# Seven half-size products for eight in the down projection of one decoder step

## The chip, the core and the metric

The kernel runs on one core of a Trainium2 chip. Its engines work side by side, each through its own queue in order: TensorE (PE) multiplies matrices into the accumulation memory PSUM; VectorE (DVE) and ScalarE (ACT) do element-wise work and can read PSUM; GpSimd (POOL) does element-wise work between tiles of the on-chip memory SBUF; SyncE (SP) issues the transfers (DMA). The metric is the time of one execution on the device in microseconds (us), from three runs for the kernel before.

## The reference

One layer of a hybrid decoder: a combined input projection, sparse attention and a recurrent branch, an output projection with a first layer norm, and then the feed-forward part, in which the change lies. There are 1032 tokens (1024 of the prompt, 8 of the sample), 1024 channels and 4096 hidden units:

```python
x1 = _layer_norm(DN_ALPHA * x + mix, ln1_g, ln1_b)
hid = jnp.square(jax.nn.relu(x1 @ w_up + b_up))
x2 = _layer_norm(DN_ALPHA * x1 + hid @ w_down + b_down, ln2_g, ln2_b)
```

The products are wanted in nearly full float32 precision. The kernel splits each operand into a high part in the shorter format that PE multiplies (fp32r) and a low part, and forms high·high + high·low + low·high: three matmuls for each one of the mathematics.

## The kernel before

Channels and hidden units lie on the 128 partitions, tokens along the free dimension. The feed-forward part (functions `g_mlw` and `g_mlp`) goes through 16 chunks of 256 hidden units. A chunk's weights are two tiles of w_up and two of w_down, 512 KB each; `g_mlw` loads each into a buffer `raw`, ACT writes its high part (L2226) and POOL its low part (L401 in the helper `gtt`, which cuts a row into four pieces of 256). They land in `wm`, one tile per chunk, in two places that take turns, so that a chunk's weights are prepared while the chunk before it is multiplied.

The tokens are cut into three groups of 384, 384 and 264 (`GROUPS`). `up` (L2249) multiplies, for one group and one half `f` of the chunk's hidden units, eight slices of the input by three products, 24 matmuls in one PSUM bank (L2260 to L2262). ACT applies bias and relu (L2266), DVE squares (L2269), ACT takes the high part of the hidden values (`hh`, L2273) and DVE the low part (`hl`, L2277). `down` (L2282) forms for one group and one slice `m` of 128 output channels six matmuls (two halves by three products, L2293 to L2295) in a bank, and DVE adds the bank to the running sum `MX` in SBUF (L2304). A chunk so has 144 matmuls up and 144 down, and 24 additions. The last chunk has groups of its own (`LAST`), and the second layer norm (`g_ln2`) runs behind it; its tiles lie in `late`.

The order on every engine is made before the run by a planner in the kernel (class `Weave`): each stream yields chains of operations with a cost on an engine and with the buffers they take and give back, and the planner emits, one by one, the operation that can start first, with a bonus per stream to break near ties. Four banks (`mm`) serve `up` and `down`; two double banks (`pr`, tiles named `pair`) serve transposes. What it emits is fixed: at run time every engine works its list off in order, and an instruction that waits holds back all behind it.

## Time and profile before

| what | value |
|---|---|
| median of 3 runs | 1443.86 us (1443.5 to 1445.07) |
| profiled execution | 1449.08 us, span from first to last instruction 1447.3 us |
| PE, DVE, ACT, POOL busy over the span | 95%, 60%, 44%, 36% |
| mean granted clock of PE | 0.986 of full speed |
| feed-forward part | first matmul at 693.1 us, chunk 15 from 1373.4 us, last matmul at 1431.4 us |

The span counts from the first instruction to the last; the remaining 1.8 us lie around it. PE is shown by its recorded instructions, whose ends are modelled: one matmul's record overlaps the next one's, so the distance between two starts is what a matmul costs, not its recorded length. The records of the other engines also run a little past the point where the next instruction can start.

### The profile page before, as it was taken

To read this page: it belongs to the slowest core of one execution; us is meant where nothing else is said; L and a number is where in the kernel's file an instruction comes from. 1 tells how busy PE (TensorE), PEld (TensorE's weight loads), DVE (VectorE), ACT (ScalarE), POOL (GpSimd) and SP (SyncE) were. 2 spreads that over 40 slices of the span, in tenths; PEclk is the share of its full clock that TensorE was granted. 3 is DMA by queue.
4 is the path that set the end of the run, shared out by engine and by line. 5 is a ranking of instruction groups with operands and counts; after the bars stand their busy time and mean duration, and the time that the engine had idled before them with its cause. 6 is when DMAs were issued, how large, how long until landed. Compare 5 with 4: busy or idle time off the path is not lost.

```text
span 1447.3 us, 24305 instructions
## 1 busy us (share of the span) xinstructions
PE 1377.3 (95%) x9529; PEld 1278.7 (88%) x9529; DVE 862.1 (60%) x1969; ACT 635.1 (44%) x1206; POOL 518.7 (36%) x675
## 2 busy tenths in 40 slices
PE   8999998899889998999999999999999999999995
PEld 7987787789876776768999999999999999999995
DVE  7388877688988578658744433344333443334457
ACT  5377998788334566556521122211222112221123
POOL 1213645454316685432431133311333113331124
PEclk9999999999999999999999999999999999999998
DMA  6122431013224353241111111111111111111012
GB/s 216 54 79 66 145 83 42 18 44 101 76 86 134 113 161 104 89 146 60 59 45 31 43 59 59 44 31 43 59 59 45 31 44 58 59 44 32 16 57 89
DMA packets 39380, 102.17 MB, mean 71 GB/s; under 512 B 6441, under 2 KB 11865, under 8 KB 39137
## 3 DMA queue, kind: packets, MB, share of 16 engines
q1 hardware_dynamic: 34144, 83.83, 17.9%
q0 software_dynamic: 5120, 16.78, 4.0%
q8 instruction: 75, 1.23, 0.4%
q14 instruction: 41, 0.33, 0.1%
HBM read 87.55 MB, written 14.62 MB: 71 GB/s over the span
## 4 chain that ended last, share of the span: by engine, by line
PE 76%; DVE 12%; ACT 7%; issue 3%; DMA 1%; POOL 1%; SPq 0%; another core or an unknown queue 0%; DVEq 0%; ACTq 0%; POOLq 0%
PE bank L2260 8%; PE bank L2261 8%; PE bank L2262 8%; PE bank L2295 8%; PE bank L2293 8%; PE bank L2294 8%; PE bank L532 4%; PE bank L533 3%; PE bank L534 3%; ACT jka L1239 3%; PE pair L1932 3%; PE bank L2032 2%; PE bank L1993 2%; DVE SC L693 2%; DVE late L2397 1%
## 5 line engine op out<-in xcount | busy, mean ns | idle before, releaser
L401 POOL TENSOR_TENSOR wm<-raw,wm 128x256 fp32r<-128x256 f32 x256 | 198.8, 807 | 481.9 <-ACT wm L2226 481.8
L2304 DVE TENSOR_TENSOR MX<-MX,bank 128x384 f32<-128x384 f32 (+2 forms) x352 | 178.6, 508 | 132.7 <-PE bank L2295 129.9
L2260 PE MATMUL bank<-X1H,wm 128*128 128x384 f32 (+2 forms) x784 | 248.2, 317 | 0.8 <-DVE MX L2304 0.8
L2261 PE MATMUL bank<-X1L,wm 128*128 128x384 f32 (+2 forms) x784 | 248.2, 317 | 0.0
L2262 PE MATMUL bank<-X1H,wm 128*128 128x384 f32 (+2 forms) x784 | 248.0, 316 | 0.0
L2293 PE MATMUL bank<-hh,wm 128*128 128x384 f32 (+2 forms) x752 | 239.4, 318 | 0.0
L2295 PE MATMUL bank<-hh,wm 128*128 128x384 f32 (+2 forms) x752 | 239.1, 318 | 0.0
L2294 PE MATMUL bank<-hl,wm 128*128 128x384 f32 (+2 forms) x752 | 238.5, 317 | 0.0
L532 PE MATMUL bank<-XH,wh 128*128 128x384 f32 (+1 forms) x600 | 200.9, 335 | 10.3 <-DVE kbs L1137 8.5
L2226 ACT ACTIVATE wm<-raw 128x1024 fp32r<-128x1024 f32 x64 | 66.9, 1050 | 296.4 <-PE bank L2295 296.4
L533 PE MATMUL bank<-XL,wh 128*128 128x384 f32 (+1 forms) x600 | 194.0, 323 | 0.8 <-DVE XL L477 0.8
L534 PE MATMUL bank<-XH,wl 128*128 128x384 f32 (+1 forms) x600 | 193.6, 323 | 0.2 <-DVE wl L513 0.2
L2269 DVE TENSOR_TENSOR r<-r 128x384 f32<-128x384 f32 (+2 forms) x98 | 53.6, 547 | 207.0 <-ACT r L2266 207.0
L2260 PEld LDWEIGHTS bank<-X1H,wm 128*128 128x128 f32 x784 | 147.5, 188 | 1.2 <-DVE MX L2304 1.0
L2262 PEld LDWEIGHTS bank<-X1H,wm 128*128 128x128 f32 x784 | 147.4, 188 | 0.0
L2261 PEld LDWEIGHTS bank<-X1L,wm 128*128 128x128 f32 x784 | 147.1, 188 | 0.0
L2294 PEld LDWEIGHTS bank<-hl,wm 128*128 128x128 f32 x752 | 141.8, 189 | 0.0
L2293 PEld LDWEIGHTS bank<-hh,wm 128*128 128x128 f32 x752 | 141.3, 188 | 0.0
L2295 PEld LDWEIGHTS bank<-hh,wm 128*128 128x128 f32 x752 | 141.2, 188 | 0.0
L2266 ACT ACTIVATE r<-bank,pvt 128x384 f32<-128x384 f32 (+2 forms) x98 | 52.9, 541 | 196.7 <-PE bank L2262 196.7
L532 PEld LDWEIGHTS bank<-XH,wh 128*128 128x128 f32 x600 | 114.6, 191 | 21.4 <-DVE kbs L1137 12.2
L401 POOL TENSOR_TENSOR wl<-raw,wh 128x256 fp32r<-128x256 f32 x92 | 77.5, 872 | 148.9 <-ACT wh L509 144.0
(419 smaller groups left out, 2491.9 us busy)
## 6 DMA issues: line engine op xcount, KB each, us to landing
raw<-in_wup SPq DMA_DIRECT2D x32, 512.0 KB
raw<-in_wdown SPq DMA_DIRECT2D x32, 512.0 KB
raw<-in_win SPq DMA_DIRECT2D x25, 512.0 KB
raw<-in_wout SPq DMA_DIRECT2D x8, 512.0 KB
zo<-in_x SPq DMA_DIRECT2D x16, 256.0 KB
zsc<-zo SPq DMA_DIRECT2D x16, 256.0 KB
z<-zsc SPq DMA_DIRECT2D x16, 256.0 KB
out_y<-late SPq DMA_DIRECT2D x16, 256.0 KB
```

The costliest lines, as they stand in the source:

```text
L401: G.tensor_tensor(out=out[:, c0:c1], in0=in0[:, c0:c1], in1=in1[:, c0:c1], op=op)
L532: T.matmul(ps[:, :n], wh[:, k, :], XH[:, k, c0:c0 + n], start=(k == 0), stop=False)
L533: T.matmul(ps[:, :n], wh[:, k, :], XL[:, k, c0:c0 + n], start=False, stop=False)
L534: T.matmul(ps[:, :n], wl[:, k, :], XH[:, k, c0:c0 + n], start=False, stop=(k == KT - 1))
L2226: S.activation(out=wts[c][:, 2 * i, 0:1024], in_=b2["f"], func=AF.Copy)
L2260: T.matmul(ps[:, :n], wh, X1H[:, k, c0:c0 + n], start=(k == 0), stop=False)
L2261: T.matmul(ps[:, :n], wh, X1L[:, k, c0:c0 + n], start=False, stop=False)
L2262: T.matmul(ps[:, :n], wl, X1H[:, k, c0:c0 + n], start=False, stop=(k == KT - 1))
L2293: T.matmul(ps[:, :n], wh, hh[:, :n], start=(f == 0), stop=False)
L2294: T.matmul(ps[:, :n], wh, hl[:, :n], start=False, stop=False)
L2295: T.matmul(ps[:, :n], wl, hh[:, :n], start=False, stop=(f == 1))
L2304: V.tensor_tensor(out=acc, in0=acc, in1=b2["ps"][:, :n], op=OP.add)
```

## The change

For chunks 1 to 14 the down product of a chunk, a 1024×256 by 256×1032 product, is taken as a 2×2 block product: w_down of the chunk is cut into A11, A12, A21, A22 (by output channels in two halves of 512 and by the two hidden halves of 128), the hidden values into B11, B12, B21, B22 (by hidden half and by tokens in two halves of 516). Eight block products would give the four result blocks; the changed kernel forms seven, A11·B11, A12·B21, S1·T1, S2·T2, S3·T3, S4·B22 and A22·T4, where S1 = A21 + A22, S2 = S1 − A11, S3 = A11 − A21, S4 = A12 − S2, and T1 to T4 are such differences of the B blocks. The sums S are made by DVE in place in the two `raw` buffers, a step of a chain that also splits all seven weight blocks (`g_mla`); the sums T are made by DVE in place in the hidden tiles `R` (`g_b`). A product has four slices `m` of 128 output channels, each of six matmuls of 258 columns into one double bank (`g_down`, L2434). Its result is added by DVE (L2446) into one of seven accumulators: four are blocks of `MX`, three (`ex`, E0 to E2) lie in the place of one weight tile; S1·T1 is added to two of them. Only after chunk 14 are the accumulators put together, by six additions of 2064 elements (`g_comb`, L2478).

Around it: the up product of these chunks uses three equal token groups of 344 and is cut in four pieces, between which the planner may set other matmuls; the up weights have one place in the place of two, so that a chunk's weights follow the ones before into the same rows when those are done; w_down blocks go through six rows that are given on from block to block (`ar`); a bank is read into two `R` tiles where it lies across the middle of the tokens. The second layer norm's parameters are loaded after the combination.

```diff
+        ST = range(1, NCH - 1)
+        NH = NT // 2
+        NG = NH // 2
+        UG = [(0, 344), (344, 344), (688, 344)]
...
+            yield "dn0"
+            for c in ST:
+                if 1 < c < ST[-1]:
+                    yield f"wt{c + 1}0"
...
+                return ([_op("SP", 0.12, l0, ["ra", "rb"]), _op("DMA", _dma(1048576))] + split_("A22", "22") + add("22", "21", "22", OP.add)
+                        + split_("S1", "22") + add("21", "11", "21", OP.subtract) + split_("A11", "11") + add("22", "22", "11", OP.subtract)
+                        + add("11", "12", "22", OP.subtract) + split_("S4", "11") + split_("S3", "21", ["rb"])
+                        + split_("A12", "12") + split_("S2", "22", ["ra"]))
...
+            prod = {"T1": ("R01", "R00"), "T3": ("R11", "R01"), "T2": ("R11", "R00"), "T4": ("R10", "R11")}.get(nme)
...
+                    for x, (w, b) in enumerate(((wh, bh), (wh, bl), (wl, bh))):
+                        for g in range(2):
+                            T.matmul(b2["pt"][:, g, 0:NG], w, b[:, g * NG:(g + 1) * NG], start=(x == 0), stop=(x == 2))
...
+                for A, B, w in (("A11", "B11", "E0"), ("A12", "B21", "11"), ("S1", "T1", ""), ("S4", "B22", "12"), ("S3", "T3", "E2"), ("S2", "T2", "E1"), ("A22", "T4", "21")):
...
+            for waits, ch in ((("dE0", "d11"), add(lambda: q(0, 0), e[0], "c11")), (("dE1",), add(e[1], e[0], "u2")),
+                              (("u2", "d12"), add(lambda: q(0, 1), e[1], "c12")), (("u2", "dE2"), add(e[2], e[1], "u3")),
+                              (("u3", "d22"), add(lambda: q(1, 1), e[2], "c22")), (("u3", "d21"), add(lambda: q(1, 0), e[2], "c21"))):
```

Up to the first up product of chunk 0 every engine's list is as before. In chunk 12, on PE, the down product before is a run of six matmuls per bank, with four banks taking turns (`hh`, `hl` are the hidden values, `wm` the weights):

```order
L2293 MATMUL bank_13126<-hh_12946,wm_12494 128x384 [waits Activation_49]
L2294 MATMUL bank_13126<-hl_12947,wm_12494 128x384
L2295 MATMUL bank_13126<-hh_12946,wm_12494 128x384
L2293 MATMUL bank_13126<-hh_12984,wm_12494 128x384
L2294 MATMUL bank_13126<-hl_12985,wm_12494 128x384
L2295 MATMUL bank_13126<-hh_12984,wm_12494 128x384
L2293 MATMUL bank_13134<-hh_12946,wm_12494 128x384 [waits DVE_49]
```

After, these are the slices 1 and 2 of chunk 9's product S2·T2, in a run of nine slices without an up product between; chunks 6 and 12 have the same run there (`bh`, `bl` are the parts of a B or T block):

```order
L2434 MATMUL pair_12642<-bh_12402,wm_7251 128x258 [waits DVE_49]
L2434 MATMUL pair_12642<-bh_12402,wm_7251 128x258
L2434 MATMUL pair_12642<-bl_12403,wm_7251 128x258 x2
L2434 MATMUL pair_12642<-bh_12402,wm_7251 128x258 x2
L2434 MATMUL pair_12650<-bh_12402,wm_7251 128x258 [waits DVE_49]
L2434 MATMUL pair_12650<-bh_12402,wm_7251 128x258
L2434 MATMUL pair_12650<-bl_12403,wm_7251 128x258 x2
L2434 MATMUL pair_12650<-bh_12402,wm_7251 128x258 x2
```

Each slice now waits for DVE to have emptied the double bank of the slice before the last: two places take turns where four did. Elsewhere most slices stand in twos with one piece of an up product (six matmuls of 344) between.

On DVE, the down product of chunk 13 before begins so (additions of banks among the last squares and subtractions of the up product):

```order
L2277 TENSOR_TENSOR hl_13506<-r_13502,hh_13505 128x264 [waits Activation_49]
L2269 TENSOR_TENSOR r_13516<-r_13516 128x264 [waits Activation_49]
L2304 TENSOR_TENSOR MX<-MX,bank_13509 128x384 [waits PE_49]
L2277 TENSOR_TENSOR hl_13527<-r_13516,hh_13526 128x264 [waits Activation_49]
L2304 TENSOR_TENSOR MX<-MX,bank_13519 128x384 [waits PE_49]
L2304 TENSOR_TENSOR MX<-MX,bank_13531 128x384 [waits PE_49]
```

After, where the hidden values of chunk 8 become complete while its first product A11·B11 is added (L2446), DVE has these in a row (L2534 squares, L2388 forms a T, L2401 forms a low part):

```order
L2446 TENSOR_TENSOR ex_7879<-ex_7879,pair_11852 128x516 [waits PE_49]
L2534 TENSOR_TENSOR r_11812<-r_11812 128x344 [waits Activation_49]
L2401 TENSOR_TENSOR bl_11880<-r_11812,bh_11879 128x516 [waits Activation_49]
L2388 TENSOR_TENSOR r_11531<-r_11812,r_11531 128x516
L2388 TENSOR_TENSOR r_11812<-r_11812,r_11487 128x516 [waits DVE_49]
L2401 TENSOR_TENSOR bl_11908<-r_11531,bh_11907 128x516 [waits Activation_49]
L2401 TENSOR_TENSOR bl_11911<-r_11812,bh_11910 128x516 [waits Activation_49]
L2388 TENSOR_TENSOR r_11728<-r_11728,r_11812 128x516
L2446 TENSOR_TENSOR ex_7879<-ex_7879,pair_11872 128x516 [waits PE_49]
L2401 TENSOR_TENSOR bl_11942<-r_11728,bh_11941 128x516 [waits Activation_49]
L2446 TENSOR_TENSOR ex_7879<-ex_7879,pair_11882 128x516 [waits PE_49]
```

Seven instructions between tiles in SBUF now stand between two additions that empty double banks; in the rows before it is one.

After chunk 14, on DVE, four of the six closing additions (L2478, 2064 elements each) stand between the additions of PE's products:

```order
L2446 TENSOR_TENSOR ex_7879<-ex_7879,pair_15009 128x516 [waits PE_49]
L2478 TENSOR_TENSOR ex_7879<-ex_7879 128x2064 [waits DVE_49]
L2478 TENSOR_TENSOR MX<-MX,ex_7879 128x4x516 [waits DVE_49]
L2478 TENSOR_TENSOR ex_7879<-ex_7879 128x2064
L2478 TENSOR_TENSOR MX<-MX,ex_7879 128x4x516 [waits DVE_49]
L2446 TENSOR_TENSOR MX<-MX,pair_15017 128x516 [waits PE_49]
```

The last of them empties the double bank that a later slice of the last product A22·T4 needs; the kernel before had no such additions.

## Rows read from the trace of the kernel before

**Rows 1.** The page, section 1: busy time, share of the span, instructions.
```profile
PE 1377.3 (95%) x9529; PEld 1278.7 (88%) x9529; DVE 862.1 (60%) x1969; ACT 635.1 (44%) x1206; POOL 518.7 (36%) x675
```

**Rows 2.** Busy time by stretch; the first line names the columns.
```profile
core 0: us, PE busy (x) PEld busy (x) DVE busy (x) ACT busy (x) POOL busy (x), PEclk, DMA share, GB/s
...
1020.00:1065.00 45.00, 45.00 (x289) 45.00 (x288) 18.65 (x36) 10.04 (x16) 12.10 (x16) 1.00 0.15 48
...
1410.00:1448.00 38.00, 21.80 (x143) 19.23 (x141) 29.42 (x49) 11.54 (x21) 18.00 (x13) 0.83 0.24 91
```

**Rows 3.** The chain that ended last, by engine.
```profile
PE 76%; DVE 12%; ACT 7%; issue 3%; DMA 1%; POOL 1%; SPq 0%; another core or an unknown queue 0%; DVEq 0%; ACTq 0%; POOLq 0%
```

**Rows 4.** Timeline of ACT: start, length, what; first weight split of chunks 5 and 6.
```profile
921.22 1.06 ACT L2226 ACTIVATE wm<-raw 128x1024 fp32r<-128x1024 f32 x1 [21.18 <-PE bank L2295]
...
966.47 1.06 ACT L2226 ACTIVATE wm<-raw 128x1024 fp32r<-128x1024 f32 x1 [21.18 <-PE bank L2295]
```

**Rows 5.** Timeline of PE: start, length; first matmul of three stretches of chunk 7.
```profile
1011.47 0.34 PE L2260 MATMUL bank<-X1H,wm 128*128 128x384 f32 x1
...
1028.25 0.28 PE L2260 MATMUL bank<-X1H,wm 128*128 128x264 f32 x1
...
1034.12 0.34 PE L2293 MATMUL bank<-hh,wm 128*128 128x384 f32 x1
```

**Rows 6.** Groups by line and shape, chunk 7 (1020 to 1065): count, busy, mean ns.
```profile
L2304 DVE TENSOR_TENSOR MX<-MX,bank 128x384 f32<-128x384 f32 x16 | 8.9, 554 | 7.1 <-PE bank L2295 6.9
...
L2304 DVE TENSOR_TENSOR MX<-MX,bank 128x264 f32<-128x264 f32 x8 | 3.4, 429 | 2.3 <-PE bank L2295 2.3
...
L2273 ACT ACTIVATE hh<-r 128x384 fp32r<-128x384 f32 x4 | 2.1, 522 | 1.9 <-DVE r L2269 1.9
...
L2273 ACT ACTIVATE hh<-r 128x264 fp32r<-128x264 f32 x2 | 0.9, 426 | 1.0 <-DVE r L2269 1.0
...
L401 POOL TENSOR_TENSOR wm<-raw,wm 128x256 fp32r<-128x256 f32 x16 | 12.4, 802 | 32.9 <-ACT wm L2226 32.9
```

**Rows 7.** Timeline of DVE: two instructions one behind the other.
```profile
990.13 0.56 DVE L2304 TENSOR_TENSOR MX<-MX,bank 128x384 f32<-128x384 f32 x1
990.60 0.43 DVE L2277 TENSOR_TENSOR hl<-r,hh 128x264 fp32r<-128x264 f32 x1
```

**Rows 8.** Timelines of PE and DVE: a product's last matmul, its addition.
```profile
1005.46 0.34 PE L2295 MATMUL bank<-hh,wm 128*128 128x384 f32 x1
...
1005.83 0.56 DVE L2304 TENSOR_TENSOR MX<-MX,bank 128x384 f32<-128x384 f32 x1 [0.49 <-PE bank L2295]
```

**Rows 9.** Timeline of SP and ACT: issue of two weight loads, read of the first.
```profile
925.19 5.33 SPq L2222 DMA_DIRECT2D raw<-in_wdown  x2
...
931.26 1.05 ACT L2226 ACTIVATE wm<-raw 128x1024 fp32r<-128x1024 f32 x1
```

**Rows 10.** Shortest, median and longest of three lines of DVE.
```profile
L2277 DVE TENSOR_TENSOR hl<-r,hh x98: 405/557/1097, 709.3 to 1414.4; 128x384 fp32r<-128x384 f32 x60, 128x264 fp32r<-128x264 f32 x32, 128x256 fp32r<-128x256 f32 x6
...
L2269 DVE TENSOR_TENSOR r<-r x98: 405/558/1451, 705.4 to 1413.4; 128x384 f32<-128x384 f32 x60, 128x264 f32<-128x264 f32 x32, 128x256 f32<-128x256 f32 x6
...
L2124 DVE TENSOR_TENSOR z<-z,bank x18: 676/686/689, 639.9 to 693.3; 128x512 f32<-128x512 f32 x16, 8x512 f32<-8x512 f32 x2
```

**Rows 11.** Timelines of DVE and POOL: a subtraction that starts during a POOL run.
```profile
1017.89 0.79 DVE L2277 TENSOR_TENSOR hl<-r,hh 128x384 fp32r<-128x384 f32 x1 [0.80 <-ACT hh L2273]
...
1017.53 3.13 POOL L401 TENSOR_TENSOR wm<-raw,wm 128x256 fp32r<-128x256 f32 x4 [1.87 <-ACT wm L2226]
```

**Rows 12.** Timelines of PE and DVE: chunk 15 begins; last matmul, last DVE group.
```profile
1373.44 0.28 PE L2260 MATMUL bank<-X1H,wm 128*128 128x264 f32 x1
...
1431.40 0.40 PE L2366 MATMUL bank<-wm,hh 128*128 128x512 f32 x1
...
1438.34 5.46 DVE L2397 TENSOR_TENSOR late<-late 128x512 f32<-128x512 f32 x5
```

More of the change, by code (lines that the diff above doesn't have):

```diff
@@ L2225, in l1 @@
                 def l1():
[L2226 removed]
+                    S.activation(out=rows()[0][:, 0:1024], in_=b2["f"], func=AF.Copy)
                 def l2():
[L2229 removed]
+                    gtt(out=rows()[1][:, 0:1024], in0=b2["f"], in1=rows()[0][:, 0:1024].bitcast(F32), op=OP.subtract)
                     W.fire(f"wt{c}{i}")
[L2231 removed]
@@ L2232, in g_mlw @@
-            for c in range(NCH):
-                if c == 1:
-                    for i in range(9):
-                        yield f"om{i}"
-                elif c:
-                    yield f"dn{c - 2}"
-                for i in range(4):
-                    yield chain(c, i), 1
-            yield f"dn{NCH - 2}"
+                rw = "raw" if c == 0 else ("rb", "ra", "ra", "rb")[i]
+                return [_op("SP", 0.06, l0, [rw]), _op("DMA", _dma(524288)), _op("ACT", _a(1024), l1), _op("POOL", _pt4(1024), l2, [], [rw])]
@@ new lines, in g_mlw, with l @@
+            for i in range(4):
+                yield chain(0, i), 1
+            for i in range(4):
+                yield f"wt0{i}"
+            for i in range(9):
+                yield f"om{i}"
+            def l():
+                ex["e"] = p0.tile([P, 6, NT], F32, name=nm("ex"), tag="XHa")
+                ex["a"] = p0.tile([P, 2, NT], F32R, name=nm("ar"), tag="XHb")
+                W.fire("ex")
+            yield [_op("SP", 0.01, l)], 1
+            for c in range(1, NCH):
+                for i in range(2):
+                    yield f"up{c - 1}{i}"
+                    if c == NCH - 1 and i == 0:
+                        yield f"ld{ST[-1]}"
+                    yield chain(c, i), 1
@@ new lines, in g_mlw @@
+            prod = {"A11": "B11", "A12": "B21", "S1": "T1", "S4": "B22", "S3": "T3", "S2": "T2", "A22": "T4"}
+            last = {x: max(list(prod).index(n) for n in prod if ar[NCH - 2][n] in x) for x in ((0, 1), (2, 3))}
+            for x, i in sorted((((0, 1), 2), ((2, 3), 3)), key=lambda y: last[y[0]]):
+                for n in list(prod)[:last[x] + 1]:
+                    yield f"P{prod[n]}{NCH - 2}"
+                yield chain(NCH - 1, i), 1
+            for nme in ("T3", "T4"):
+                yield f"P{nme}{NCH - 2}"
@@ L2242, in ld @@
+            for q in ("11", "12", "21", "22"):
+                yield f"c{q}"
             def ld():
-                late["t"] = p0.tile([P, 8, NT], F32, name="late", tag="XL")
+                late["t"] = rows8("late", F32)
                 for r in range(2):
@@ new lines, in build, with g_comb, q, add @@
+        B_DS = 0.5
+        def g_comb():
+            def q(r, cc):
+                return MX[:, 4 * r:4 * r + 4, cc * NH:(cc + 1) * NH]
+            def add(o, x, ev):
+                def f(eng):
+                    if eng == "DVE":
+                        V.tensor_tensor(out=o(), in0=o(), in1=x(), op=OP.add)
+                    else:
+                        for m in range(4):
+                            gtt(out=o()[:, m], in0=o()[:, m], in1=x()[:, m], op=OP.add, parts=2)
+                    W.fire(ev)
+                return [_op("DVE", _d1(4 * NH), lambda: f("DVE"))]
+            e = [lambda k=k: eacc(k) for k in range(3)]
+            for waits, ch in ((("dE0", "d11"), add(lambda: q(0, 0), e[0], "c11")), (("dE1",), add(e[1], e[0], "u2")),
+                              (("u2", "d12"), add(lambda: q(0, 1), e[1], "c12")), (("u2", "dE2"), add(e[2], e[1], "u3")),
+                              (("u3", "d22"), add(lambda: q(1, 1), e[2], "c22")), (("u3", "d21"), add(lambda: q(1, 0), e[2], "c21"))):
+                for w in waits:
+                    yield w
+                yield ch, 1
@@ L2428, in g_ln2 @@
                 if gi in TM:
-                    for g in range(3):
-                        if g0 < sum(GROUPS[g]) and GROUPS[g][0] < g0 + gn:
-                            yield f"acc{g}"
+                    for q in ("11", "12", "21", "22"):
+                        yield f"c{q}"
                     for f in range(2):
```

279 lines of the change are left out of this document (234 added, 45 removed).

## The prediction

> **What bounds the kernel now.** I read the busy shares first, then the windows of the feed-forward part, then single lines in the timelines. PE is busy for 95% of the span and DVE for 60% [rows 1]. The average hides the stages, so one chunk is looked at by itself: from 1020 to 1065 us PE is busy for the whole 45 us at a granted clock of 1.00, beside 18.7 us of DVE, 10.0 of ACT and 12.1 of POOL [rows 2]. PE is the bound there, with no gap that another engine would have to close, and 76% of the chain that ended last lies on it [rows 3]. The first weight split of chunk 6 comes 45.25 us after that of chunk 5 [rows 4], and this is the time of a chunk. Only the end is different: from 1410 us PE is busy for 21.8 of 38 us and DVE for 29.4 [rows 2].
>
> The sum is made against the profiled execution, 1449.1 us (span 1447.3 and 1.8 around it). The median is 5.2 us lower; I carry this distance to the result unchanged.
>
> **The PE term.** What a matmul costs is the distance between starts. In chunk 7 the first 96 up matmuls (384 columns) take 16.78 us, 0.1748 each, and the next 48 (264 columns) 5.87 us, 0.1223 each [rows 5]. The slope is 0.0525 us for 120 columns, 0.4375 ns for one. An up product of three groups of 344 has 144 matmuls of 0.1573, 22.65 us, which is what 96 and 48 give now (22.65). Down now takes 45.25 − 22.65 = 22.6 us. After, it is 168 matmuls of 258 columns; on the line they cost 0.1197 each, 20.11 us. The gain is 2.49 us per chunk, 34.9 for 14 chunks. Above, it is bounded by pure columns, a seventh product less in eight: 22.6 / 8 = 2.83, or 39.6 us. Below, a matmul of 258 columns costs no less than the one of 264 if that stands on a floor already (0.1223): 20.55 us, a gain of 2.05 or 28.7 us. I take 34.9, since two points 120 columns apart show no floor.
>
> **What it adds on the other engines.** A DVE addition of 384 columns has a record of 554 ns, one of 264 has 429 [rows 6]: 1.04 ns per column, so 691 ns for 516. Two that follow at once start 0.47 us apart where the record has 0.56 [rows 7], so a pitch is the record less 0.085: 0.606. A chunk has 32 bank additions (19.4), 11 operations on the B and T blocks (6.7), 4 on the sums of A (2.4) and 8 squares (2.7): 31.2 us of the some 43 that it would last, 73% where DVE had 41%. ACT, at 522 and 426 ns for the same two widths [rows 6], comes to some 14 us, and POOL with 22 pieces in the place of 16, at 3.13 us for four [rows 11], to 17.2. None is the bound by its sum. What they cost is waits, because every list is fixed, and only two double banks take the products.
>
> *The first product of chunk 1* needs its weights prepared from the load on: at most 6.1 us of load, since a load issued at 925.19 was read at 931.26 [rows 9], three splits of half a tile (0.63 on ACT and 1.56 on POOL, 2.2 each) and two sums of 0.69: 14.1 us. Fifteen up pieces of 6 × 0.157 = 0.94 us lie beside it, 14.1. I take 2 us, range 0 to 4. In later chunks the same chain and the up weights' split ahead of it have some 20 us of slices and pieces beside them and need 17, so nothing is taken.
>
> *Slices without an up piece between.* A slice costs PE 0.72. DVE started the addition 0.37 us after the start of the last matmul of a product, 0.20 after that matmul's pitch [rows 8]. A double bank so turns round in 0.72 + 0.20 + 0.69 and some 0.05, 1.65 us for every two slices, which PE would do in 1.43. That is 0.12 us on each of some 51 slices that come third or later in a row without a piece: 6 us, range 0 to 12.
>
> *S1·T1 has two additions per slice*: eight, 4.85 us of DVE, beside four slices (2.9) and two or three pieces (1.9 to 2.8). DVE just keeps up, and a square or a low part in between makes a double bank late. I take 0.25 per chunk, 3.5 us; range 0 to 14, the upper end being 1 us, the time that one addition and a square delay the next slice.
>
> *The row of seven operations on DVE* (square, low parts and T blocks), once per chunk, between additions of A11·B11. From the end of the up group, through ACT, square, the seven and the addition behind them, it takes some 7.5 us (relu 0.5, seven pitches near 0.6 each, three waits for ACT's high part of 0.6, the addition 0.7). PE has 8.5 us of work before it needs that bank: two slices, a piece, two slices, five pieces. So it is hidden with 1 us to spare, if nothing stretches it. What can is POOL. While POOL split a weight, a subtraction that usually takes 0.56 took 0.79 [rows 11], and single ones of the two SBUF lines took 1.10 and 1.45 [rows 10]; the additions that read a bank of PSUM and one SBUF tile never did (L2124: 676 to 689 in 18). A chunk will have 23 operations that read two SBUF operands, where it had 12. I take 0.4 us per chunk, 5.6 in all; range 0 to 21, at 1.5 per chunk, when two or three pieces of POOL (0.78) are waited out.
>
> The Trainium skill ("SBUF — State Buffer", section "Who interferes with whom") says that a DVE instruction with two SBUF inputs and a GpSimd instruction that reads SBUF hold a shared port as an exclusive lock, so the second one waits until the first is done, and that a DVE instruction with at most one SBUF input does not contend. The trace agrees in kind: 0.79 for 0.56 [rows 11], and the PSUM line without a stretch [rows 10]; the 0.23 us seen there is less than a whole piece of 0.78. Taken at an average half piece for those that meet POOL (17.2 of 43 us), the rule would add 23 × 0.4 × 0.39 = 3.6 us of DVE per chunk, 34.8 in all, still below PE's 42.8.
>
> *The closing additions.* 2064 columns at 1.04 ns and 0.07 of pitch, 2.2 us each, 13.3 for six. Four stand between the additions of chunk 14's last slices: with the additions at either side some 10.5 us of DVE, before the double bank is free that slice 2 of A22·T4 needs. PE has some 7.8 us of work beside it (two slices and nine pieces of 264 or 256 columns). A stall of 2.7; range 0 to 5.
>
> *The end.* Chunk 15 begins at 1373.44 and PE ends at 1431.40, 58 us, with 16 more to the end on DVE [rows 12]. This part has the same products; its order is another, and the last two closing additions (4.4 us) lie in it beside PE's up products. I take 0, range −4 to 4. The clock in the feed-forward part stays at 1.00 in the sum; in the end, with PE half busy, it was 0.83 [rows 2].
>
> **The sum.** 34.9 − 2 − 6 − 3.5 − 5.6 − 2.7 = 15.1. 1449.1 − 15.1 = 1434.0 for a profiled run, 1428.8 as a median: 1429.
>
> **Rivals.** *The cover holds almost everywhere.* Banks, T blocks and POOL all come in time, and only the start of chunk 1 and the closing additions cost. For it: DVE has 27% to spare, and the trace shows few stretched operations. Against: two banks in turn, on fixed lists. 34.9 − 4.7 and some 3 of scattered waits: 1449.1 − 27 = 1422, a median of 1417; at the bound of pure columns with no wait 1404.
>
> *Waits in order eat most of the gain.* The slices and S1·T1 at the upper ends (12 and 14), the row of seven as taken: 34.9 − 2 − 12 − 14 − 5.6 − 2.7 = −1.4, and with half of that more, 6 us gained. For it: 73% of DVE in a fixed order is where short queues begin to show. A median of 1436 to 1444.
>
> *Slower: POOL holds up DVE where PE waits for it.* The place is the row of seven and the six or eight operations (sums of A, squares, low part) ahead of it, 13 or more with two SBUF operands, while POOL splits the blocks of A at the same time, so that here the meeting is not by chance. The price is a piece of 0.78 each time. With 1 us of spare per chunk, four such waits leave 2.1 us on PE, 29.6 for 14 chunks: 34.9 − 2 − 6 − 3.5 − 29.6 − 2.7 = −8.9, 1458, a median of 1453. It decides from 1.5 us on PE per chunk, 2.5 us of waits, a little over three pieces. Against it: the stretch seen is 0.23, and half of the operations wait for ACT or DMA anyway. If all 23 waited for a whole piece, DVE would have 49.1 us per chunk and be the bound itself.
>
> **How the numbers follow.** Below 0.2% (2.9 us) a difference in this kernel can't be told from none: faster is below 1441, slower above 1446.7. The forecast has 0.50, with its own range of 1420 to 1438; the cover that holds 0.18; waits that eat most 0.19, of which 0.06 lie within 0.2% of before; the slower case 0.13. Faster so has 0.50 + 0.18 + 0.13 = 0.81, same 0.06, slower 0.13. The range for 8 in 10 leaves out the slower case and the edge of pure columns: 1409 to 1445.
>
> **What would show it.** The first up matmuls of successive chunks stand 43 to 44 us apart, where 45.25 is now; below 43 the cover held, above 45 a rival is right. Starts of matmuls of 258 columns in a slice stand 0.12 apart; at 0.1223 or more there is a floor. PE's idle time lies ahead of the slices (L2434) and is ended by DVE's additions (L2446), most in runs without a piece and behind S1·T1. DVE's low parts, T blocks and sums of A (L2401, L2388, L2358) are longer than 0.69 where POOL works. Behind chunk 14 the four long additions stand ahead of a wait of PE of 2 to 3 us. The forecast is wrong if PE waits for weights (ACT or POOL) in each chunk, if the clock falls in the feed-forward part, or if DVE is busy for over 36 us of a chunk.

## The result: slower, and the profile after

The changed kernel takes 1466.59 us (median of 4 runs, 1465.41 to 1467.53), the kernel before 1443.68 in the same runs: a ratio of 1.0157, 95% interval 1.0139 to 1.0175. The forecast was 1429, with a range of 1409 to 1445; it was wrong in sign. The profiled execution has a span of 1464.6 us.

The page of the changed kernel, section 1 (busy time, share of the span, instructions), against [rows 1]:

```profile
PE 1370.7 (94%) x9865; PEld 1254.8 (86%) x9865; DVE 1120.7 (77%) x2239; ACT 685.3 (47%) x1318; POOL 594.2 (41%) x761
```

PE has only 6.6 us less to do by these records, and DVE 258.6 more. The engine of the chain says where the time went; DVE has 20% of it where it had 12% [rows 3]:

```profile
PE 64%; DVE 20%; ACT 8%; issue 3%; DMA 2%; POOL 1%; SPq 0%; DVEq 0%; ACTq 0%; POOLq 0%
```

Busy time by stretch (one chunk from the middle; the closing additions; the end):

```profile
core 0: us, PE busy (x) PEld busy (x) DVE busy (x) ACT busy (x) POOL busy (x), PEclk, DMA share, GB/s
...
1057.00:1102.50 45.50, 43.99 (x313) 43.17 (x313) 37.60 (x58) 14.34 (x25) 18.04 (x22) 1.00 0.15 46
...
1388.00:1400.00 12.00, 9.22 (x72) 9.01 (x72) 11.46 (x10) 1.71 (x4) 0.00 (x0) 0.94 0.00 1
...
1438.00:1450.00 12.00, 5.83 (x21) 4.51 (x20) 8.16 (x16) 3.62 (x7) 5.30 (x4) 0.72 0.25 92
```

Where PE was busy for all of 45 us [rows 2], it now has holes: 1.5 us in these 45.5. The granted clock is still 1.00 (2.4 GHz), so the clock is not the cause in the middle. In chunk 14 and at the end it is a part of it: the trace has a granted clock of 0.50 (1.2 GHz) for 3.4 us from 1374.7, for 3.4 from 1398.6 and for 6.8 from 1443.0, each time close behind a stretch in which PE stood still for 2 to 4 us; in the feed-forward part before, it was 1.00 up to the last matmul. DVE is busy for 37.6 of 45.5 us, over the 36 that the prediction named as a sign that it is wrong. The first up matmuls of chunks 5 and 14 are 408.9 us apart (901.6 to 1310.5), 45.43 per chunk, where it was 45.25 [rows 4].

The timeline of PE (start, length, engine, line; in brackets the idle time before it and its releaser) shows one hole, in chunk 7, ahead of the third slice of A12·B21, and below it the cost of matmuls that wait for nothing:

```profile
1046.14 0.32 PE L2509 MATMUL bank<-X1L,wm 128*128 128x344 f32 x1
...
1046.77 0.32 PE L2510 MATMUL bank<-X1H,wm 128*128 128x344 f32 x1
1048.35 0.51 PE L2434 MATMUL pair<-bh,ar 128*128 128x258 f32 x2 [1.26 <-DVE MX L2446]
...
1051.30 0.65 PE L2434 MATMUL pair<-bh,wm 128*128 128x258 f32 x4
1051.79 0.40 PE L2434 MATMUL pair<-bl,wm 128*128 128x258 f32 x2
```

The timeline of DVE in the same place says what PE waited for:

```profile
1039.88 0.69 DVE L2401 TENSOR_TENSOR bl<-r,bh 128x516 fp32r<-128x516 f32 x1
1040.49 2.38 DVE L2388 TENSOR_TENSOR r<-r,r 128x516 f32<-128x516 f32 x2
1042.79 0.68 DVE L2401 TENSOR_TENSOR bl<-r,bh 128x516 fp32r<-128x516 f32 x1
1043.39 0.68 DVE L2446 TENSOR_TENSOR ex<-ex,pair 128x516 f32<-128x516 f32 x1
1044.00 0.68 DVE L2401 TENSOR_TENSOR bl<-r,bh 128x516 fp32r<-128x516 f32 x1
1044.60 1.24 DVE L2388 TENSOR_TENSOR r<-r,r 128x516 f32<-128x516 f32 x1
...
1046.54 1.15 DVE L2401 TENSOR_TENSOR bl<-r,bh 128x516 fp32r<-128x516 f32 x1 [0.70 <-ACT bh L2396]
1047.61 1.28 DVE L2446 TENSOR_TENSOR MX<-MX,pair 128x516 f32<-128x516 f32 x2
```

And the timeline of POOL says why three T sums (L2388; 2.38 us for two, and 1.24) and a low part (L2401, 1.15) are long, where others last 0.69:

```profile
1040.03 2.29 POOL L416 TENSOR_TENSOR wm<-raw,wm 128x256 fp32r<-128x256 f32 x2 [0.67 <-PE pair L2434]
...
1042.99 2.30 POOL L416 TENSOR_TENSOR ar<-raw,ar 128x256 fp32r<-128x256 f32 x2 [0.68 <-ACT ar L2349]
1045.25 1.89 POOL L416 TENSOR_TENSOR wm<-raw,wm 128x256 fp32r<-128x256 f32 x2
```

Each long one overlaps a POOL run, and POOL's pieces, 0.74 us as the median, are longer beside them too (2.30 for two). Not every overlap is long on DVE: the low part at 1044.00 took 0.68. Over the whole kernel, shortest, median and longest of three lines of DVE (ns), against [rows 10]:

```profile
L2388 DVE TENSOR_TENSOR r<-r,r x56: 689/1120/1251, 751.6 to 1371.2; 128x516 f32<-128x516 f32 x56
...
L2401 DVE TENSOR_TENSOR bl<-r,bh x98: 680/697/1243, 747.9 to 1372.5; 128x516 fp32r<-128x516 f32 x98
...
L2446 DVE TENSOR_TENSOR MX<-MX,pair x280: 677/691/695, 764.9 to 1400.0; 128x516 f32<-128x516 f32 x140
```

Of the T sums 35 of 56 are stretched, the same three of four in each of chunks 4 to 13; the 280 additions that read a bank never are. In the rows above POOL's splits of weights and DVE's sums on B stand in the same few us, and the lists repeat this from chunk to chunk.

**The account.** The feed-forward part, first product to end, lasted 754.2 us before (the same in both traces of that kernel) and lasts 773.1 after: 18.9 more. By places, from the starts of PE's matmuls in the trace (a wait is what a start comes later than the usual distance): fewer matmuls −32.1 (2.3 per chunk, 14 chunks); waits in chunks 3 to 13 +26.7 (2.4 each); in chunks 1 and 2 +8.6; in chunk 14 +9.2; chunk 15 and the end +6.5, which is what remains. In the last two places some 5.4 us are matmuls at half the clock, an estimate from their starts (258 columns 0.215 us apart, where it is 0.121). Ahead of the feed-forward part 3.3 are lost as well. The sum is 22, beside 22.4 between the two spans and 22.9 between the medians.

### The profile page after: what moved, and what is told of

Its sections match the earlier page's. It is cut to its first block, busy times and chain, and to the rows that moved or that the text cites. A ratio compares the mean times of both kernels' runs of the same rounds, so it can differ in the third digit from the quotient of the medians.

```text
span 1464.6 us, 25643 instructions
## 1 busy us (share of the span) xinstructions
PE 1370.7 (94%) x9865; PEld 1254.8 (86%) x9865; DVE 1120.7 (77%) x2239; ACT 685.3 (47%) x1318; POOL 594.2 (41%) x761
## 3 DMA queue, kind: packets, MB, share of 16 engines
q8 instruction: 78, 1.28, 0.4%
## 4 chain that ended last, share of the span: by engine, by line
PE 64%; DVE 20%; ACT 8%; issue 3%; DMA 2%; POOL 1%; SPq 0%; DVEq 0%; ACTq 0%; POOLq 0%
PE pair L2434 18%; PE bank L2508 6%; PE bank L2510 6%; PE bank L2509 6%; PE bank L557 3%; ACT jka L1264 3%; PE bank L558 3%; PE bank L559 3%; DVE r L2388 3%; PE pair L1957 3%; PE bank L2057 2%; DVE bl L2401 2%; DVE SC L718 2%; PE bank L2018 2%; DVE MX L2446 1%
## 5 line engine op out<-in xcount | busy, mean ns | idle before, releaser
L2508 PE MATMUL bank<-X1H,wm 128*128 128x344 f32 (+3 forms) x784 | 249.5, 318 | 0.0
L2510 PE MATMUL bank<-X1H,wm 128*128 128x344 f32 (+3 forms) x784 | 248.6, 317 | 0.0
L2509 PE MATMUL bank<-X1L,wm 128*128 128x344 f32 (+3 forms) x784 | 248.3, 317 | 0.0
L2446 DVE TENSOR_TENSOR MX<-MX,pair 128x516 f32<-128x516 f32 x280 | 185.3, 688 | 41.3 <-PE pair L2434 39.3
L2434 PE MATMUL pair<-bh,wm 128*128 128x258 f32 x1040 | 201.2, 291 | 15.9 <-DVE MX L2446 11.1
L2434 PEld LDWEIGHTS pair<-bh,wm 128*128 128x128 f32 x1040 | 159.2, 190 | 27.0 <-DVE MX L2446 11.7
L2446 DVE TENSOR_TENSOR ex<-ex,pair 128x516 f32<-128x516 f32 x156 | 106.9, 690 | 33.3 <-PE pair L2434 31.3
L558 PEld LDWEIGHTS bank<-XL,wh 128*128 128x128 f32 x600 | 114.9, 191 | 1.6 <-DVE XL L502 1.2
L559 PEld LDWEIGHTS bank<-XH,wl 128*128 128x128 f32 x600 | 114.5, 191 | 0.1
L2434 PE MATMUL pair<-bh,ar 128*128 128x258 f32 x528 | 100.0, 288 | 9.3 <-DVE MX L2446 6.7
L2434 PE MATMUL pair<-bl,wm 128*128 128x258 f32 x520 | 105.7, 285 | 0.0
```

The costliest lines, as they stand in the source:

```text
L558: T.matmul(ps[:, :n], wh[:, k, :], XL[:, k, c0:c0 + n], start=False, stop=False)
L559: T.matmul(ps[:, :n], wl[:, k, :], XH[:, k, c0:c0 + n], start=False, stop=(k == KT - 1))
L2434: T.matmul(b2["pt"][:, g, 0:NG], w, b[:, g * NG:(g + 1) * NG], start=(x == 0), stop=(x == 2))
L2446: V.tensor_tensor(out=o, in0=o, in1=src_, op=OP.add)
L2508: T.matmul(ps[:, :n], wh, X1H[:, k, c0:c0 + n], start=(k == 0), stop=False)
L2509: T.matmul(ps[:, :n], wh, X1L[:, k, c0:c0 + n], start=False, stop=False)
```

## Experiments

Theory A: POOL's weight splits stretch DVE's sums of B blocks and, through the fixed list, make PE's double banks late. Rival B: the lists themselves, with two double banks and 37 us of DVE per chunk, make the waits whatever POOL does. Rival C: the closing additions carry most of it. Each ratio below is to the kernel before, measured along with that kernel (medians of 1443.7 to 1447.0); a difference in us to the changed kernel is one between such groups of runs.

**POOL's low parts left out.** In chunks 2 to 13 the low parts of the A blocks and of the up weights are not formed; every other instruction and every list stays.

```diff
-    gtt(out=row[:, 512:1024], in0=b2[at], in1=row[:, 0:512].bitcast(F32), op=OP.subtract, parts=2)
+    if not 2 <= c <= 13:        # the same for the up weights
+        gtt(out=row[:, 512:1024], in0=b2[at], in1=row[:, 0:512].bitcast(F32), op=OP.subtract, parts=2)
```

> The changed kernel with the same order of instructions on PE, DVE, ACT and SP; POOL's low parts of the up weights and of the blocks of A are left out in chunks 2 to 13 (what was there before is read). Theory A (POOL stretches DVE's operations with two SBUF operands, 0.54 us each, and the row of seven at A11·B11 makes the double banks late): the T sums (L2388) fall from a median of 1.12 us to 0.69, PE's wait ahead of A12·B21 from 1.3 to 1.6 per chunk to under 0.4, a chunk from 45.4 to some 43.7, and the time from 1466.6 by 15 to 21 us to about 1448. Theory B (the row of seven and two double banks alone, whatever POOL does): the wait stays above 1.0 and the time above 1460.

Measured: 1446.26 us, 1.0005 of before (0.9996 to 1.0015), 20.3 below the changed kernel. Its T sums, and its middle chunk by stretch:

```profile
L2390 DVE TENSOR_TENSOR r<-r,r x56: 683/694/1116, 751.8 to 1351.1; 128x516 f32<-128x516 f32 x56
```

```profile
1057.00:1100.70 43.70, 43.68 (x315) 43.36 (x314) 33.19 (x55) 13.59 (x24) 0.00 (x0) 1.00 0.16 50
```

With POOL silent, DVE has 33.2 us of work in the place of 37.6, PE no hole, the wait at A12·B21 is 0 in chunks 3 to 13 and a chunk takes 43.72. The lists are the same, so B falls for this wait: it is A. The waits of chunks 3 to 13 fall from 26.7 to 9.6 us, those of chunks 1 and 2 from 8.6 to 5.5, together 20.3, as much as the time. What is left there, slices without an up piece above all, is the lists' own, and so is chunk 14, whose waits stay (9.6). What the seven products bring is then used up by these waits, the end and what lies ahead: the feed-forward part takes 752.8 us, where it was 754.2.

**Smaller POOL pieces.** Pieces of 128 columns in the place of 256.

```diff
+    gtt(..., parts=8 if c in ST else 4)      # up weights, was 4
+    gtt(..., parts=4)                        # A blocks, was 2
```

> The changed kernel with the same order of instructions; POOL's low parts of the up weights and of A (chunks 1 to 14) are cut into pieces of 128 columns in the place of 256, so twice as many and each shorter. If DVE waits for a whole piece of POOL to end (theory A as a lock): the stretch of a T sum falls from 0.54 to some 0.3, PE's wait ahead of A12·B21 from 1.5 to some 0.8, time 1455 to 1462. If the two share bandwidth for as long as both work: the stretch stays at 0.5 and the time within 2 us of 1466.6. If POOL's longer total time (some 20 us per chunk for 16) makes weights late: PE waits for POOL and the time is above 1468.

Measured: 1459.62, 1.0100 (1.0084 to 1.0117), 7.0 below the changed kernel.

```profile
L2388 DVE TENSOR_TENSOR r<-r,r x56: 682/842/969, 750.7 to 1364.6; 128x516 f32<-128x516 f32 x56
```

POOL's piece falls from 0.74 to 0.46 us, the T sum's stretch from 0.42 or 0.54 us to 0.15 or 0.27. What DVE loses follows the length of POOL's piece: the piece is shorter by 0.28, the stretch by 0.27. The wait at A12·B21 falls to about 1 us and the chunk to 44.85. This supports A with a size, not only with an on and off.

**Closing additions left out.** The six additions are not made; their event fires at once.

```diff
-    return [_op("DVE", _d1(4 * NH), lambda: f("DVE"))]
+    return [_op("DVE", _d1(4 * NH), lambda: W.fire(ev))]
```

> The changed kernel with the same order; the six closing additions of 2064 elements after chunk 14 are left out. By theory A only what they cost at the end goes: the wait of 3.0 ahead of slice 2 of chunk 14's last product, and a part of the two that stand among chunk 15's operations: 3.4 to 9 us, about 1460. If the end is late for another reason (the order of chunk 15 and of the second layer norm): less than 4 us, 1463 or more.

Measured: 1458.93, 1.0099 (1.0082 to 1.0116), 7.7 below. The waits of chunk 14 fall from 9.2 to 3.9 us, and the feed-forward part is 6.5 shorter; the rest of the 7.7 lies ahead of it. C is a part, a third of what A is. The waits of the middle chunks stay (26.7). In the changed kernel DVE's timeline shows the four in a row, and PE's the wait behind them:

```profile
1387.81 2.31 DVE L2478 TENSOR_TENSOR ex<-ex 128x2064 f32<-128x2064 f32 x1
1390.15 2.31 DVE L2478 TENSOR_TENSOR MX<-MX,ex 128x2064 f32<-128x2064 f32 x1
1392.38 2.30 DVE L2478 TENSOR_TENSOR ex<-ex 128x2064 f32<-128x2064 f32 x1
1394.72 2.31 DVE L2478 TENSOR_TENSOR MX<-MX,ex 128x2064 f32<-128x2064 f32 x1
1396.94 1.29 DVE L2446 TENSOR_TENSOR MX<-MX,pair 128x516 f32<-128x516 f32 x2
```

```profile
1397.68 0.51 PE L2434 MATMUL pair<-bh,ar 128*128 128x258 f32 x2 [2.78 <-DVE MX L2446]
```

**Squares on ACT.** The squares of the hidden values move from DVE to ACT.

```diff
-    V.tensor_tensor(out=r, in0=r, in1=r, op=OP.mult)
+    S.activation(out=r, in_=r, func=AF.Square)
...
-    ... _op("DVE", _d1(n) + x, sv)]
+    ... _op("ACT", _a(n) + x, sv)]
```

> The changed kernel with the squares of chunks 1 to 14 made by ACT (8 per chunk, half of ACT's time is free) in the place of DVE; the planner orders anew. DVE has 8 operations of two SBUF operands fewer, 2.7 us without a stretch and some 4.5 with it. Theory A: the operations that stand ahead of the additions are one of seven fewer, PE's wait at A12·B21 falls by 0.5 to 1.0 per chunk, time 1452 to 1460. Theory B (DVE is held by T and low parts in a row): the same wait, within 4 us of 1466.6.

Measured: 1471.41, 1.0178 (1.0161 to 1.0195), 4.8 above the changed kernel, with intervals that overlap: a miss for both theories. DVE has less work, but the planner has made another order, with chunks of 40.8 and 51.3 us in turn. PE's waits are 0.7 to 1.0 us in the odd chunks from 3 to 13 and 5.4 to 5.6 in the even ones, 32.1 in all (26.7 in the changed kernel). The longest stands ahead of A12·B21, in chunk 8 here, and ends on ACT, which splits the block A12 just then:

```profile
1098.85 0.51 PE L2434 MATMUL pair<-bh,wm 128*128 128x258 f32 x2 [1.68 <-ACT wm L2349]
```

```profile
1098.18 0.61 ACT L2349 ACTIVATE wm<-raw 128x512 fp32r<-128x512 f32 x1
```

So less work on DVE did not shorten the program: the new order makes a weight late in every second chunk. An edit that changes the lists tests two things at once; the first two experiments, which kept them, are the ones that tell.

**The planner told the stretched costs.** If the planner plans with the time that a T sum has beside POOL, it should leave room.

```diff
-    return [_op("DVE", _d1(512), ...)]
+    return [_op("DVE", _d1(512) + 0.1, ...)]                               # sums of A
+    ct, cl = {"DVE": _d1(NH) + 0.43}, {"DVE": _d1(NH) + 0.06}              # T sums, low parts
-    ... _op("DVE", _d1(n) + x, sv)]
+    ... _op("DVE", _d1(n) + x + 0.12, sv)]                                 # squares
```

> The changed kernel, with the planner told what DVE's operations with two SBUF operands took beside POOL: 0.43 us more for a T sum, 0.06 for a low part, 0.12 for a square, 0.1 for a sum of A. Nothing is left out; from chunk 6 on the planner's list is the same in each chunk, and no product runs through without up pieces (before, every third chunk had eight slices so). Theory A (the planner's list was made for unstretched operations, so the additions behind the row come late): PE's wait at A12·B21 falls from 1.5 to under 0.5 and that of the dense slices (1.3 in every third chunk) goes; 1.2 to 2.0 per chunk on 11 chunks, 1445 to 1455. Theory B (DVE is simply too full and what is moved comes back as another wait): 1460 or more.

Measured: 1448.91, 1.0033 (1.0020 to 1.0046), 17.7 below the changed kernel, the largest gain of an edit that computes everything. A middle chunk:

```profile
1067.00:1110.00 43.00, 42.91 (x310) 42.39 (x309) 37.43 (x55) 13.62 (x24) 18.09 (x22) 1.00 0.14 50
...
1340.00:1356.00 16.00, 9.75 (x63) 9.45 (x63) 15.18 (x20) 3.76 (x6) 5.43 (x6) 0.81 0.29 99
```

DVE still has 37.4 us of work per chunk; the sums are stretched as before, but no longer where PE is waiting: a chunk takes 43.73 on the mean of chunks 5 to 13, 43.55 in the later ones. This limits A: the stretch costs PE only where the list puts it in front of a bank. The second row is what is left: in chunk 14 PE idles for 6.5 us behind this stretch of DVE, a closing addition and then a row of six ahead of the addition that frees the bank:

```profile
1341.94 2.31 DVE L2479 TENSOR_TENSOR MX<-MX,ex 128x2064 f32<-128x2064 f32 x1
1344.17 0.69 DVE L2401 TENSOR_TENSOR bl<-r,bh 128x516 fp32r<-128x516 f32 x1
1344.77 1.42 DVE L2388 TENSOR_TENSOR r<-r,r 128x516 f32<-128x516 f32 x2
1346.16 2.30 DVE L2401 TENSOR_TENSOR bl<-r,bh 128x516 fp32r<-128x516 f32 x2
1348.38 1.21 DVE L2388 TENSOR_TENSOR r<-r,r 128x516 f32<-128x516 f32 x1
1349.52 0.68 DVE L2447 TENSOR_TENSOR MX<-MX,pair 128x516 f32<-128x516 f32 x1
```

The granted clock over these 16 us is 0.81, and behind the hole matmuls of 258 columns start 0.21 to 0.22 us apart until 1356.6, at half speed (1.2 GHz).

**Both, and parts.** Costs and 128-column pieces together, with the planner's extra costs set to the shorter stretch (0.22 for a T sum):

> As f1, with POOL's pieces cut to 128 columns (a stretch of some 0.25) and the planner's extra costs set to that (0.22, 0.12, 0.1, 0.08). If both causes add up, the chunk comes near PE's own 43.1: 43.2 to 43.7, and the time to 1440 to 1450. If the smaller pieces only help where the row is late, it equals f1 within 3 us.

Measured: 1449.32 (1.0033, 1.0020 to 1.0045), the same as with the costs alone: the two are not additive. The wait at A12·B21 is down to some 0.5 us with the costs alone and gone here; this plan has another in its place, 0.7 to 1.7 us at S1·T1 in each of chunks 4 to 13. The costs differ between the two, so the lists do too, and which of the two edits does what is not shown.

The closing additions in four parts of 516, each on DVE or POOL, alone, and then with the two others:

```diff
-    return [_op("DVE", _d1(4 * NH), lambda: f("DVE"))]
+    return [_op("DVE|POOL", {"DVE": _d1(NH), "POOL": _pt4(NH, 2)}, lambda e, m=m: f(m, e)) for m in range(4)]
```

> The changed kernel, with each closing addition cut into its four slices of 516, which the planner may set on DVE or POOL; the rest of the planner's costs as in the changed kernel. Of the 7.7 us that the closing additions were worth (run without them), 3 to 6 come back, since a bank addition no longer stands behind four times 2.2 us and POOL is idle there: 1460.5 to 1463.5. If POOL's additions stretch DVE's instead: within 1 us of 1466.6 or above.

> f2 with the closing additions in parts as in f3. If the three are independent: f2 less 3 to 6 us, so 1436 to 1447, and near or below the kernel before (1443.7). If the end is set by the second layer norm and not by the closing additions: f2 within 2 us.

Measured: 1469.39 (1.0178, 1.0161 to 1.0195) and 1452.71 (1.0055, 1.0038 to 1.0072), 2.8 above the changed kernel (with intervals that overlap) and 3.4 above the kernel with costs and 128-column pieces: misses. In the first, the wait at S1·T1 in chunk 14 becomes 7.9 us; in both, the stretch from the last matmul to the end is 12.7 in the place of 10.0. That smaller parts let the planner put more of them early, since it has no notion that they are not urgent, is argued and not shown.

**Closing additions late.** Costs as above, the additions in parts on DVE, and their bonus from 1.0 to −0.5; the second kernel also with 128-column pieces (and +0.12 for a low part).

```diff
- ("mlp", 1.0, g_comb())
+ ("mlp", -0.5, g_comb())
```

> f1 (planner told of the stretch), with each closing addition cut into four of 516 on DVE and the closing stream's bonus taken from 1.0 to -0.5, so that it is set only where nothing else can start. In f1 chunk 14 waits 11.5 us, 7.0 of it ahead of slice 2 of S1·T1, where a closing addition of 2.3 us and the row of six stood ahead of a bank addition. If that closing addition causes it: the wait falls by 2.3 to 4 and the 2.5 at A22·T4 goes, 1448.9 less 4 to 7, so 1442 to 1445. If the row of six alone does it: 1446 to 1449. The bank additions that the closing ones are set behind may make the end later: then no gain.

> g1 with POOL's pieces of 128 columns (each stretch 0.25 in the place of 0.54) and the planner's extra costs left at those of 256, so that real time is below the planned one. If waits come where reality is later than the plan, hardly any is left within a chunk: 43.1 to 43.4 per chunk for f1's 43.55, 2 to 6 us below g1. If POOL's 19 us per chunk or the plan's own gaps decide: g1 within 2 us.

Measured: 1449.38 (1.0036, 1.0024 to 1.0049) and 1457.05 (1.0089, 1.0072 to 1.0106). In the first, chunk 14's waits fall from 11.8 to 6.0 us, but the end takes the gain back. In the second a chunk takes 44.73, for another reason than before: PE waits 1.4 us at S1·T1 in each of chunks 5 to 13, for a bank addition. Timelines of POOL, SP, ACT and DVE ahead of it, one chunk:

```profile
1083.70 2.17 POOL L416 TENSOR_TENSOR ar<-raw,ar 128x128 fp32r<-128x128 f32 x4
...
1085.90 0.80 SPq L2278 DMA_DIRECT2D raw<-in_wup  x2
...
1089.58 1.06 ACT L2282 ACTIVATE wm<-raw 128x1024 fp32r<-128x1024 f32 x1 [3.90 <-DMA raw<-in_wup]
1090.54 0.62 ACT L2396 ACTIVATE bh<-r 128x516 fp32r<-128x516 f32 x1
...
1091.19 0.95 DVE L2401 TENSOR_TENSOR bl<-r,bh 128x516 fp32r<-128x516 f32 x1 [1.34 <-ACT bh L2396]
```

A weight split waits for its DMA; the high part behind it on ACT, the low part on DVE and the bank's addition wait with it. The DMA was issued when POOL had ended its last piece on the `raw` buffer that it fills. POOL takes 8.0 us for the last three A blocks in pieces of 128 columns, from 1077.87, and 6.7 in the first kernel with pieces of 256, and there the same DMA is issued 1.1 us earlier in its chunk. So shorter pieces have a price of their own, a longer POOL run, and the list makes PE pay it here; the lists of the two kernels differ, so what each contributes is not shown.

**Costs only for chunks 3 to 13, and the kernel before once more.** The first keeps chunks 1, 2 and 14 planned as in the change (closing parts on DVE, bonus 0). The second is the kernel before, unchanged, for a second trace.

> As g1, but the planner's extra costs hold for chunks 3 to 13 alone, where they helped, and the closing stream's bonus is 0; chunks 1, 2 and 14 keep the changed kernel's list but for the closing additions in parts. In f1 chunk 2 lost 7.8 us and chunk 14 11.5, in the changed kernel 5.9 and 9.3. If the costs were wrong there and right between: 1448.9 less 2 and less 2 to 5, 1442 to 1445, even with the kernel before. If the end takes back what chunk 14 gives, as in g1: 1446 to 1449.

> The kernel before, unchanged, for a second trace. Its profiled execution was 5.2 us over its median, that of the changed kernel 0.2 under. If a profile costs this kernel some 5 us each time, the span is 1446 to 1448 again; if the first one was a chance, 1442 to 1444, and the difference lies in one stretch of the trace.

Measured: 1448.32 (1.0033, 1.0023 to 1.0043), chunks of 43.69 on the mean of chunks 5 to 13, with 0.5 to 0.6 of waits in each of chunks 4 to 13. The kernel before took 1443.97 with a span of 1442.2, and its feed-forward part 754.2 us as in the first trace; the 5.1 us by which the first trace was longer lie wholly ahead of it. So the sum of the prediction started from an execution that by chance was long in an earlier stage; the distance to the median was carried unchanged and so did no harm.

**Turns of buffers.** Ahead of the feed-forward part the lists are as before, and yet 3.3 us are lost. ACT's timeline after, and in the second trace of before, behind the same instruction:

```profile
654.76 1.52 ACT L2198 ACTIVATE z<-z,sd 128x512 f32<-128x512 f32 x2 [0.99 <-DVE sd L2122]
662.46 0.63 ACT L2139 ACTIVATE mh<-MX 128x512 fp32r<-128x512 f32 x1 [6.18 <-PE bank L2152]
```

```profile
654.59 1.52 ACT L2161 ACTIVATE z<-z,sd 128x512 f32<-128x512 f32 x2 [0.99 <-DVE sd L2085]
656.02 0.61 ACT L2102 ACTIVATE mh<-MX 128x512 fp32r<-128x512 f32 x1
```

The change gives these tiles their places in another turn, so that one falls on a buffer that a matmul still reads. The test gives them the turn of before by a list of places, with the same instructions:

```diff
+ first = [0, 1, 2, 3, 4, 5, 0, 1, 2, 3, 4, 5, 4, 5, 0, 1, ...]
+ if tag == "ml" and first:
+     k = first.pop(0)
```

> The changed kernel with all five lists unchanged; only the places of the tiles mh, ml, x1 and r of the output projection, the first layer norm and chunk 0 (six places) are given out in the turn that the kernel before has. In the changed kernel ACT stood idle for 6.2 us ahead of a split of mh (L2139) at 656 to 662 us, until PE had read the place it writes, and the feed-forward part began 3.1 us later after the same point than before. If the turn of places is the cause: the wait goes, and the time falls by 3.1 us, to 1463.5. If it is something else that the list holds back: within 1 us of 1466.6.

> h1 (planner told of the stretch in chunks 3 to 13, closing additions in parts) with the places given out as in i1. h1 had 753.7 us from the first up product to the end, the kernel before 754.2 in both of its traces. With the 3.1 us ahead of it gone as well the two are equal: 1443 to 1446, ratio 0.999 to 1.001. If the places don't matter: 1448.

> i2 without the closing additions in parts (they stay whole and early, as in the changed kernel). If parts are worth something here, unlike in f3: 2 to 5 us above i2. If the end takes it back: within 1.5 us of i2.

Measured: with the changed kernel's lists 1469.06, beside 1447.03 for the kernel before on that chip (its 23 runs spread from 1444.0 to 1452.3): 1.0138 (1.0117 to 1.0159). The interval overlaps that of the change, so by the median it is open; the trace shows the wait gone, and the stretch between the same two matmuls of PE 45.8 us long, where it was 45.7 before and 49.0 after:

```profile
661.41 1.52 ACT L2201 ACTIVATE z<-z,sd 128x512 f32<-128x512 f32 x2 [0.99 <-DVE sd L2125]
662.83 0.62 ACT L2142 ACTIVATE mh<-MX 128x512 fp32r<-128x512 f32 x1
```

With the costs for chunks 3 to 13 (and the closing additions in parts) 1449.28 (1.0016, 1.0003 to 1.0029), with the costs alone 1449.37 (1.0012, 1.0001 to 1.0023). By their ratios these are the nearest to the kernel before of all that compute everything; none is faster than it.

## Why the prediction was wrong, step by step

Between the sum (15.1 us faster than the profiled run) and the measurement (some 22 slower) lie 37 us. The terms, one by one:

*PE term*: 34.9 forecast, about 32 measured. Where nothing waits, matmuls of 258 columns start 0.1207 us apart on the mean and those of 264 0.1219, in the changed kernel and in the experiments alike. The line through 384 and 264 had 0.1197 for 258, the floor 0.1223; the value lies between. 344 columns cost 0.1575, as forecast (0.1573).

*First product of chunk 1*: 2 forecast. PE's waits in chunk 1 are 2.6 us; chunk 2, for which nothing was taken, has 6.0, in holes of up to 1.3. The longest of them ends on a weight split of ACT that was late, most of the others on DVE's additions.

*Slices without an up piece*: 0.12 a slice forecast, 0.16 measured on eight slices of every third chunk, some 5 us in all: right. *S1·T1*: 0.25 per chunk forecast, 0.05 to 0.6 measured: right in chunks 3 to 13. With POOL's low parts left out, chunks 3 to 13 have 9.6 us of waits, and 9.5 were forecast for these two over 14 chunks.

***The row of seven operations on DVE*: this is the step that failed.** "I take 0.4 us per chunk, 5.6 in all; range 0 to 21". Measured at A12·B21, the product whose bank stands behind that row: 1.28 to 1.67 us in each of chunks 4 to 13 (in chunks 5, 8 and 11 the trace names ACT's high part of the last T sum, which ended 0.07 us behind the addition), 15 us in chunks 3 to 13, and none there with POOL's low parts left out. Place and mechanism were right, and the size was wrong: leaving those low parts out gives back 20.3 us, the forecast had 5.6 for all that POOL does. In chunk 7 the row had 1 us to spare by the forecast, and four of its operations together lasted 2.0 us longer than at 0.69. Two readings led to the low value. The price was taken from one subtraction of 0.79 [rows 11], 0.23 more than usual, where an outlier of [rows 10] showed the 0.54 more (1.10 for 0.56) that became the rule; its 1.45 did not. And the meetings were taken as by chance. Over the whole chunk that was not far off: 3.6 us of DVE forecast, and 4.4 by the difference between 37.6 and the 33.2 without POOL's low parts. But 2.0 of them stand in this one row, in front of a bank, and the text's own rival said why: the chain that prepares A and the sums of B are due together, in the same order in every chunk. One meeting of a fixed list is a meeting in every chunk.

The Trainium skill ("SBUF — State Buffer", section "Who interferes with whom") says that a DVE instruction with two SBUF inputs contends with a GpSimd instruction that reads SBUF, the second of them waiting until the first is done, and that one with at most one SBUF input does not contend. The runs agree: a T sum of 0.69 becomes 1.11 to 1.25 beside pieces of 0.74, it takes 0.15 to 0.27 more beside pieces of 0.46, 694 ns as the median with POOL's low parts left out, and the bank additions, with one input in PSUM, take 676 to 695. In the changed kernel a T sum lost 0.56 at most, less than a whole piece.

*The closing additions*: 2.7 forecast; the wait named is there (2.78 by its row), but chunk 14 has 9.2 in all, 2.2 and 1.6 of the rest at S4·B22. There a row of six low parts and T sums on DVE, none of them stretched, stands ahead of the bank's addition: at this place the list makes PE wait without any stretch. *The end*: 0 (−4 to 4) forecast, +6.5: 12 us more until the last matmul, partly given back by a stretch from it to the end of 10.0 us in the place of 15.9. *Ahead of the feed-forward part*: "lists as before" was taken to mean times as before; the buffers' turn cost 3.3. *The clock*: 1.00 was taken, and the prediction named a fall as a sign that it is wrong; at half the clock some 5.4 us were lost in chunk 14 and the end, and these are part of the 9.2 and the 6.5.

So POOL's meetings are nearly 15 of the 37 us, the largest single miss, the PE term 3, and what lies at the edges beside them (chunks 1, 2 and 14, the end, and ahead) nearly 20; for most of the edges nothing had been taken.

The slower rival, with a chance of 0.13, had the right place and kind; it asked for 2.1 us on PE per chunk at the row, and 1.28 to 1.67 are there, from long operations that lose about 0.5 us each in the place of 0.78. Its 1453 fell short of 1466.6 all the same, by what lay at the edges. The other miss is one of method: the terms for waits were each taken near their low ends, each with PE's pieces between slices as its cover, and they share that one cover.

What stays open: whether the lists can be planned so that the edges also lose nothing. With the middle chunks at 43.7, the feed-forward part lasted as long as before (753.7 against 754.2), so the 17 us that chunks 3 to 13 gain against 45.25 each still go at the edges. Not tried: a third double bank.

## What to carry to other kernels

Fewer matmuls with more element-wise sums are paid in the order of the lists: where a chain repeats in each chunk, an overlap with another engine's work seen once should be priced as certain, at the long durations that the trace shows and not at a mean, and at the place in the list where it falls. Tell a planner the duration that an operation has beside the others (17.7 us here), rather than the one that it has alone, before making it cheaper (7.0 us here). And price the edges, first and last chunks, by themselves.

## What was unexpected on the hardware

- Distances between matmul starts at a granted clock of 1.00, means where nothing waits: 0.1747 us at 384 columns, 0.1575 at 344, 0.1219 at 264, 0.1207 at 258. From 344 to 264 a column is worth 0.45 ns, from 264 to 258 0.2.
- A stretch of DVE cost PE nothing by itself: with the planner's new costs 45 of 56 T sums were stretched, more than the 35 in the changed kernel, and the program was 17.7 us faster.
- Shorter POOL pieces did not always help: where the planner already had the costs, 128-column pieces went with +7.7 us in one plan (1449.38 to 1457.05, with another order of the lists) and with no change in another (1448.91 to 1449.32).
- In the changed kernel the granted clock fell to 0.50 behind holes of PE of 2.0, 2.8 and 3.9 us, and matmuls of 258 columns then started 0.215 us apart; in the middle chunks, with holes of up to 1.4 us, it stayed at 1.00.
- With the lists ahead of it unchanged, the turn in which tiles get their buffers cost ACT a wait of 6.2 us and PE 3.3.
- Two executions of the kernel before differed by 5.1 us, all of it in earlier stages; the feed-forward part was 754.2 in both.
